# A bidirectional mLSTM scan: units of two, scores in banks of their own, and three small operations for five

## The chip, the cores and the metric

The kernel is one launch on all 8 cores of one Trainium2 chip. Each core works on one sample sequence of 2048 tokens and four prompt sequences of 256 tokens. The metric is the device time of the slowest core in microseconds (us). An execution is called slow when one die (cores 0 to 3, or 4 to 7) falls behind at a lower granted clock; only fast runs are compared, or cores of an undisturbed die. TensorE is PE in the profile, VectorE is DVE, ScalarE is ACT, GpSimd is POOL.

## The reference, cut to what matters

The layer has a Hyena branch, an mLSTM branch and an MLP. The change touches the mLSTM branch alone, and there one step of its scan over chunks of 128 tokens, for each of four heads and two directions:

```python
def step(carry, inp):
    C, n, m = carry
    ...                                            # gates: b, d, m_inter, m_comb
    s = jnp.einsum('bhjd,bhsd->bhjs', qc, kc) * jnp.exp(d - m_comb[..., None])
    num = w_inter[..., None] * jnp.einsum('bhjk,bhkv->bhjv', qc, C) + jnp.einsum('bhjs,bhsv->bhjv', s, vc)
    den = w_inter * jnp.einsum('bhjk,bhk->bhj', qc, n) + jnp.sum(s, axis=-1)
    h = num / jnp.maximum(jnp.abs(den), jnp.exp(-m_comb))[..., None]
    ...                                            # m_new, w_state, decay
    C_new = decay[..., None, None] * C + jnp.einsum('bhsk,bhsv->bhkv', kc * w_state[..., None], vc)
    n_new = decay[..., None] * n + jnp.einsum('bhs,bhsk->bhk', w_state, kc)
    return (C_new, n_new, m_new), h
```

The forward and the backward result are added. A chain of such steps (C to C_new) is serial, but the eight chains of a sequence are independent of each other.

## The kernel before: the parts concerned

A "pair" is one head in one direction. A group of the scan holds two heads of the sample sequence (4 pairs, 16 chunks; two such large groups) or eight pairs of prompt sequences (2 chunks; four small groups). That makes 192 steps in all, done four pairs at a time: 48 rounds. A round, with arguments cut and comments added:

```python
for i in range(nck):
    for batch in batches:                       # four pairs
        for p, (c_, d) in enumerate(batch):     # X = XB[p], Z = ZB[p]: two PSUM banks for each pair
            ... matmul(X[:, 0:128], lhsT=kT, rhs=qT)                # scores
        for e in st:
            ... vector.scalar_tensor_tensor(out=ST, in0=X[:, 0:128], WSq, masks)
            ... scalar.activation(out=cbt, in_=cf, scale=DECq)      # Cb: the state, decayed, bf16
            ... scalar.activation(out=kw, in_=ktok, scale=WSq)
        for e in st:
            ... matmul(X[:, 128:385], lhsT=ST, rhs=vt)              # output and denominator
            ... matmul(X[:, 128:385], lhsT=qT, rhs=cbt)
            ... matmul(X[:, 386:390], lhsT=kw, rhs=vt[:, c, 255:257])
            ... matmul(Z, lhsT=kw, rhs=vt)                          # the new part of the state
        for e in st: ... vector: cf[0:256] = cf * DECq + Z          # Cf, 128x512
        for e in st: ... vector: cf[256] = cf * DECq + X[...]       # Cf, last column
        for e in st: ... vector: sc0 = X[:, 384] * U                # the five small ones
        for e in st: ... vector: sc3 = max(-sc0, sc0)
        for e in st: ... vector: sc1 = max(sc3, EN)
        for e in st: ... vector: sc2 = 1 / sc1
        for e in st: ... vector: sc3 = sc2 * U
        for e in st:
            if first touch of this chunk: ... scalar.activation(out=hacc, in_=X[:, 128:384], scale=sc3)
            else:                         ... vector: hacc = X[:, 128:384] * sc3 + hacc
```

A helper puts in every wait by buffer, and a PSUM bank is one buffer. In the first half of a sequence's chunks the accumulate (Hacc) is a first touch and runs on ScalarE; in the second half the other direction has been there, and it runs on VectorE.

## Time and profile before

| | before |
|---|---|
| median, lowest, highest | 5136.06, 5121.35, 5364.1 us in 3 runs |
| spans of the 8 cores in the profiled run | 5090.8 to 5120.6 us |
| busy share of the whole span: PE, DVE, ACT | 65%, 41%, 20% |
| scan of a large group (16 rounds) | about 164.5 us |
| scan of a small group (4 rounds) | about 41 us |
| from the first scan's start to the last one's end, over the cores | 845 to 869 us |

A group's scan is counted from its first ST to the end of its last Hacc, in the timeline; the six together take some 494 us. Between groups lie the transposes of the next heads, and the norm and the store of the last ones. The shares of the whole span say little here, as nine tenths of it belong to other stages.

### The profile page before, as it was taken

How to read it: one execution, taken by the hardware profiler on the slowest of the kernel's cores; microseconds unless marked ns; L12 is line 12 of the kernel's file. 1: busy time of each engine (PE TensorE's matmuls, PEld its weight loads, DVE VectorE, ACT ScalarE, POOL GpSimd, SP SyncE). 2: the span in 40 equal slices, each digit the busy share in tenths (PEclk: the TensorE clock that was granted, in tenths of full speed). 3: DMA queues.
4: the chain of work that ended last, by engine and by line, in shares of the span. 5: the costliest groups of instructions: out<-in, count | busy, mean ns of one | idle time of the engine just before them, and what ended most of it. 6: DMA issues, size and time to landing. Idle time of an engine off the chain costs nothing.

```text
span 5120.6 us, 56640 instructions; the slowest of 8 cores (5090.8 to 5120.6 us)
## 1 busy us (share of the span) xinstructions
PE 3353.6 (65%) x17932; PEld 1732.5 (34%) x17932; DVE 2108.2 (41%) x4215; ACT 1019.2 (20%) x1859; POOL 413.8 (8%) x449
## 2 busy tenths in 40 slices
PE   2199999905444222289938586476864795698697
PEld 1144444403222111034414454335452342343343
DVE  0332201474656343354354555454432522532532
ACT  0401132215454222132010000000000221131131
POOL 0000000000000000000003232232310000000000
PEclk7599999956666555589958788788887898899898
DMA  8444543202020332235624353354436445445542
GB/s 144 143 98 135 179 136 99 83 16 71 17 75 17 57 38 38 50 108 170 180 94 155 127 163 133 127 163 150 147 133 177 78 74 157 98 67 122 123 68 65
DMA packets 316514, 547.68 MB, mean 107 GB/s; under 512 B 31190, under 2 KB 238457, under 8 KB 305785
## 3 DMA queue, kind: packets, MB, share of 16 engines
q1 hardware_dynamic: 221424, 442.73, 27.6%
q0 software_dynamic: 94800, 101.34, 13.0%
q8 instruction: 151, 2.47, 0.2%
q14 instruction: 139, 1.14, 0.1%
HBM read 521.56 MB, written 123.76 MB: 126 GB/s over the span
## 4 chain that ended last, share of the span: by engine, by line
PE 58%; DMA 15%; DVE 14%; ACT 6%; issue 5%; SPq 2%; POOL 1%; DVEq 0%; ACTq 0%; POOLq 0%
PE bank L538 11%; PE bank L1151 7%; PE bank L1372 7%; PE bank L1387 6%; PE bank L1244 6%; DMA ogP<-s_kvo 4%; PE bank L1220 4%; PE bank L1223 3%; PE bank L565 3%; DMA ust<-s_uT 2%; SPq L151 2%; DMA ptD<-pos 2%; DMA GTc<-GTS 2%; PE bank L1354 2%; DMA wada<-w_ada 2%
## 5 line engine op out<-in xcount | busy, mean ns | idle before, releaser
L538 PE MATMUL bank<-hnT,wsl 128*128 128x512 bf16 x2688 | 580.3, 379 | 0.0
L1244 PE MATMUL bank<-GTc,Y 128*128 128x256 bf16 x3328 | 412.6, 288 | 202.4 <-DMA GTc<-GTS 130.2
L1244 PEld LDWEIGHTS bank<-GTc,Y 128*128 128x128 bf16 x3328 | 340.2, 103 | 268.2 <-issue 209.0
L538 PEld LDWEIGHTS bank<-hnT,wsl 128*128 128x128 bf16 x2688 | 262.9, 98 | 317.3 <-issue 0.4
L1151 PE MATMUL bank<-HWb,FTf 128*128 128x512 bf16 x1568 | 357.2, 385 | 3.9 <-DMA FTf<-FTP 3.9
L1372 PE MATMUL bank<-mh,wslD 128*128 128x512 bf16 x1536 | 337.8, 384 | 7.3 <-DVE mh L467 7.3
L1387 PE MATMUL bank<-wslD,f1T 128*128 128x512 bf16 x1536 | 332.0, 379 | 6.3 <-DVE f1T L1376 6.3
L1025 PE MATMUL bank<-identb,hf 128*128 128x128 bf16 x192 | 35.7, 288 | 374.9 <-DVE hf L1020 347.4
L1220 PE MATMUL bank<-ztok,FTc 128*128 128x512 bf16 x832 | 205.2, 397 | 67.3 <-DMA FTc<-FTP 34.1
L1208 ACT COPY ztok<-bank 128x512 bf16<-128x512 bf16 x96 | 54.7, 588 | 951.7 <-PE bank L1206 949.3
L1338 PE MATMUL bank<-f1T,wslD 128*128 128x512 bf16 x384 | 100.3, 408 | 180.4 <-DVE tA L1344 104.1
L1151 PEld LDWEIGHTS bank<-HWb,FTf 128*128 128x128 bf16 x1568 | 154.0, 99 | 187.4 <-issue 12.5
L1372 PEld LDWEIGHTS bank<-mh,wslD 128*128 128x128 bf16 x1536 | 151.5, 99 | 193.0 <-issue 15.8
L1387 PEld LDWEIGHTS bank<-wslD,f1T 128*128 128x128 bf16 x1536 | 150.1, 98 | 188.3 <-issue 7.7
L1376 DVE TENSOR_TENSOR f1T<-tA 128x512 bf16<-128x512 f32 x192 | 132.9, 692 | 179.3 <-ACT tA L1375 177.6
L1223 PE MATMUL bank<-ztok,FTc 128*128 128x512 bf16 x832 | 197.7, 386 | 0.0
L1248 DVE SCALAR_TENSOR_TENSOR itmp<-zc,bfm,bank 128x256 f32<-128x256 bf16 x192 | 90.9, 479 | 250.5 <-PE bank L1244 234.5
L1375 ACT ACTIVATE tA<-bank,bfm 128x512 f32<-128x512 f32 x192 | 131.9, 687 | 227.4 <-DVE f1T L1376 179.9
L957 DVE SCALAR_TENSOR_TENSOR Cf<-Cf,TSC,bank 128x512 f32<-128x512 f32 x192 | 141.5, 748 | 81.5 <-PE bank L951 60.7
L565 PE MATMUL bank<-wsl,hnT 128*128 128x512 bf16 x768 | 165.9, 379 | 0.0
L1153 DVE TENSOR_TENSOR hss<-bank,invt 128x512 bf16<-128x512 f32 x112 | 76.7, 687 | 216.5 <-PE bank L1151 215.6
L936 ACT ACTIVATE Cb<-Cf,TSC 128x514 bf16<-128x514 f32 x192 | 136.8, 713 | 77.7 <-DVE Cf L962 77.7
(228 smaller groups left out, 4441.4 us busy)
## 6 DMA issues: line engine op xcount, KB each, us to landing
FTf<-FTS SPq DMA_DIRECT2D x96, 512.0 KB, 3.8
FTc<-FTS SPq DMA_DIRECT2D x96, 512.0 KB, 4.5
GTc<-GTS SPq DMA_DIRECT2D x32, 1536.0 KB, 8.5
wslD<-w_mlp POOLq DMA_DIRECT2D x48, 1024.0 KB, 9.4
s_uT<-stF SPq DMA_DIRECT2D x24, 1536.0 KB
ust<-s_uT SPq DMA_DIRECT2D x24, 1024.0 KB
wsl<-w_in POOLq DMA_DIRECT2D x18, 1024.0 KB, 12.1
wada<-w_ada POOLq DMA_DIRECT2D x6, 2048.0 KB, 23.1
```

Of the source, the lines that this page charges most:

```text
L538: op("pe", lambda: nc.tensor.matmul(pp[:], lhsT=wt[:, k, m * 128:(m + 1) * 128], rhs=hnT[:, k, tt * 512:(tt + 1) * 512], start=(k == 0), s ...
L565: op("pe", lambda: nc.tensor.matmul(pp[:], lhsT=hnT[:, k, tk * 128:(tk + 1) * 128], rhs=wt[:, k, :], start=(k == 0), stop=(k == 7)), r=[wb ...
L936: op("act", lambda: nc.scalar.activation(out=cbt[:], in_=cf[:], func=AF.Copy, scale=S(DECq)), r=[cfb, TSC_b], w=[cbb])
L957: op("dve", lambda: nc.vector.scalar_tensor_tensor(out=cf[:, :, 0:256], in0=cf[:, :, 0:256], scalar=Sx(e, DECq), in1=Z[:, 0:512].rearrange ...
L1151: op("pe", lambda: nc.tensor.matmul(ps[:], lhsT=ft[:, tc * 128:(tc + 1) * 128], rhs=HW_[:, tc, :], start=(tc == 0), stop=(tc == nt - 1)), ...
L1220: op("pe", lambda: nc.tensor.matmul(pr_[:], lhsT=fre[:, tc * 128:(tc + 1) * 128], rhs=ztok[:, tc, :], start=(tc == 0), stop=(tc == nt - 1) ...
L1223: op("pe", lambda: nc.tensor.matmul(pi_[:], lhsT=fim[:, tc * 128:(tc + 1) * 128], rhs=ztok[:, tc, :], start=(tc == 0), stop=(tc == nt - 1) ...
L1244: op("pe", lambda: nc.tensor.matmul(ps[:, 0:256], lhsT=Y[:, fc, j * 128:(j + 1) * 128], rhs=gt[:, fc * 256:(fc + 1) * 256], start=(fc == 0 ...
L1372: op("pe", lambda: nc.tensor.matmul(ps[:], lhsT=w1t[:, k, m4 * 128:(m4 + 1) * 128], rhs=mh[:, k, ts_], start=(k == 0), stop=(k == 7)), r=[ ...
L1375: op("act", lambda: nc.scalar.activation(out=ta[:], in_=ps[:], func=AF.Relu, bias=bfm[:, BM1 + fc:BM1 + fc + 1]), r=[psb, bfm_b], w=[tab])
L1376: op("dve", lambda: nc.vector.tensor_tensor(out=f1T[:, fc, ts_], in0=ta[:], in1=ta[:], op=ALU.mult), r=[tab], w=[f1T_b])
L1387: op("pe", lambda: nc.tensor.matmul(ps[:], lhsT=f1T[:, fbk * 8 + q, i * 128:(i + 1) * 128], rhs=w2t[:, q, :], start=first, stop=last), r=[ ...
```

## The change

Its intent is to break the ring in which every engine waits for another. Scores move into two banks of their own, so that they needn't wait for the last reader of the output bank; a unit becomes two pairs; output banks alternate from one unit to the next; and the front part of unit k+1 (scores, ST, Cb, kw) is given to the engines ahead of the back part of unit k. Besides, the factor U of the small operations is taken into the floor EN beforehand, which is the same function of the same numbers: 1/max(|x|·U, EN)·U = 1/max(|x|, EN/U).

```diff
-        op("dve", ... tensor_tensor(out=FREE[:], in0=R3[:], in1=R7[:], op=ALU.add) ...)
+        op("dve", ... tensor_tensor(out=V3(FREE), in0=V3(R3), in1=bc(ML), op=ALU.add) ...)
...
-                for i in range(nck):
-                    for batch in batches:
-                        ... X=XB[p], Z=ZB[p] ...
-                        ... matmul(X[:, 0:128], ...)
+                PB = 2
+                units = [(i, pairs[b:b + PB]) for i in range(nck) for b in range(0, len(pairs), PB)]
+                def stage1(k):      # scores
+                        bp = (k % 2) * PB + p
+                        ... X=XB[bp], Z=ZB[p], S=(ZB[2 + k % 2], p * 128) ...
+                            ... matmul(S[:, s0:s0 + 128], ...)
+                def stage2(st):     # ST; all Cb; all kw
+                def stage3(st):     # the back part's matmuls
+                def stage4(st):     # Cf, last column, then
+                        ... tensor_scalar(out=sc[:, 0:1], in0=X[:, 384:385], scalar1=-1.0, op0=ALU.mult)
+                        ... scalar_tensor_tensor(out=sc[:, 1:2], in0=X[:, 384:385], scalar=EN, in1=sc[:, 0:1], op0=ALU.max, op1=ALU.max)
+                        ... reciprocal(out=sc[:, 3:4], in_=sc[:, 1:2])
+                        ... Hacc as before
+                cur = stage1(0)
+                stage2(cur)
+                for k in range(len(units)):
+                    nxt = stage1(k + 1) if k + 1 < len(units) else None
+                    stage3(cur)
+                    yield
+                    if nxt is not None:
+                        stage2(nxt)
+                    stage4(cur)
+                    yield
+                    cur = nxt
```

More of the change, by code (lines that the diff above doesn't have):

```diff
@@ L799, in _phaseB @@
         op("act", lambda: nc.scalar.activation(out=R2[:], in_=R2[:], func=AF.Exp), r=[R2b], w=[R2b])
-        op("dve", lambda: nc.vector.tensor_tensor(out=FREE[:], in0=R3[:], in1=R7[:], op=ALU.add), r=[R3b, R7b], w=[FREEb])
+        op("dve", lambda: nc.vector.tensor_tensor(out=V3(FREE), in0=V3(R3), in1=bc(ML), op=ALU.add), r=[R3b, ML_b], w=[FREEb])
         op("act", lambda: nc.scalar.activation(out=FREE[:], in_=FREE[:], func=AF.Exp, scale=-1.0), r=[FREEb], w=[FREEb])
@@ L910, in run_groups @@
                 pairs = [(c_, d) for c_ in ctx for d in range(2)]
-                batches = [pairs[b:b + bsz] for b in range(0, len(pairs), bsz)]
-                for i in range(nck):
-                    for batch in batches:
-                        st = []
-                        for p, (c_, d) in enumerate(batch):
-                            js, h, s_ = c_["js"], c_["h"], c_["s"]
-                            c = i if d == 0 else nck - 1 - i
-                            cg = c_["t0"] // 128 + c
-                            col = d * 4 + h
-                            ri = rot[0] % NR; rot[0] += 1
-                            e = dict(c=c, cg=cg, col=col, tk=slice(c * 128, (c + 1) * 128), X=XB[p], Z=ZB[p], ST=STs[ri], kw=kws[ri], sc=scs[ri],
-                                     cf=Cf[js][d], cb=Cb[js][d], s=s_, c_=c_, d=d)
-                            st.append(e)
-                            qT, qTb = s_["qT"]; kT, kTb = s_["kT"]
-                            X, Xb = e["X"]
-                            for dk in range(2):
-                                op("pe", lambda: nc.tensor.matmul(X[:, 0:128], lhsT=kT[:, dk, e["tk"]], rhs=qT[:, dk, e["tk"]], start=(dk == 0), stop=(dk == 1)),
-                                   r=[kTb, qTb], w=[Xb], inc=(dk == 1))
-                        yield
-                        for e in st:
-                            S = lambda q: TSC[:, e["cg"], q, e["col"]:e["col"] + 1]
-                            X, Xb = e["X"]; ST, STb = e["ST"]; kw, kwb = e["kw"]; cf, cfb = e["cf"]; cbt, cbb = e["cb"]
-                            ktok, ktokb = e["s"]["ktok"]
-                            op("dve", lambda: nc.vector.scalar_tensor_tensor(out=ST[:], in0=X[:, 0:128], scalar=S(WSq), in1=masks[:, e["d"], :],
-                                                                             op0=ALU.mult, op1=ALU.mult), r=[Xb, TSC_b, masks_b], w=[STb])
-                            op("act", lambda: nc.scalar.activation(out=cbt[:], in_=cf[:], func=AF.Copy, scale=S(DECq)), r=[cfb, TSC_b], w=[cbb])
-                            op("act", lambda: nc.scalar.activation(out=kw[:], in_=ktok[:, e["c"], :], func=AF.Copy, scale=S(WSq)), r=[ktokb, TSC_b], w=[kwb])
-                        yield
-                        for e in st:
-                            X, Xb = e["X"]; Z, Zb = e["Z"]; ST, STb = e["ST"]; kw, kwb = e["kw"]; cbt, cbb = e["cb"]
-                            qT, qTb = e["s"]["qT"]; vt, vtb = e["s"]["vt"]
-                            c = e["c"]
-                            op("pe", lambda: nc.tensor.matmul(X[:, 128:385], lhsT=ST[:], rhs=vt[:, c, :], start=True, stop=False), r=[STb, vtb], w=[Xb], inc=False)
-                            for dk in range(2):
-                                op("pe", lambda: nc.tensor.matmul(X[:, 128:385], lhsT=qT[:, dk, e["tk"]], rhs=cbt[:, dk, :], start=False, stop=(dk == 1)),
-                                   r=[qTb, cbb], w=[Xb], inc=False)
-                            for dk in range(2):
-                                op("pe", lambda: nc.tensor.matmul(X[:, 386 + 2 * dk:388 + 2 * dk], lhsT=kw[:, dk * 128:(dk + 1) * 128], rhs=vt[:, c, 255:257], start=True, stop=True),
-                                   r=[kwb, vtb], w=[Xb], inc=(dk == 1))
-                            for dk in range(2):
-                                op("pe", lambda: nc.tensor.matmul(Z[:, dk * 256:(dk + 1) * 256], lhsT=kw[:, dk * 128:(dk + 1) * 128], rhs=vt[:, c, 0:256], start=True, stop=True),
-                                   r=[kwb, vtb], w=[Zb], inc=(dk == 1))
-                        yield
-                        Sx = lambda e, q: TSC[:, e["cg"], q, e["col"]:e["col"] + 1]
-                        for e in st:
-                            X, Xb = e["X"]; Z, Zb = e["Z"]; cf, cfb = e["cf"]
-                            op("dve", lambda: nc.vector.scalar_tensor_tensor(out=cf[:, :, 0:256], in0=cf[:, :, 0:256], scalar=Sx(e, DECq),
-                                                                             in1=Z[:, 0:512].rearrange("p (k v) -> p k v", v=256),
-                                                                             op0=ALU.mult, op1=ALU.add), r=[Zb, TSC_b, cfb], w=[cfb])
-                        for e in st:
-                            X, Xb = e["X"]; cf, cfb = e["cf"]
-                            op("dve", lambda: nc.vector.scalar_tensor_tensor(out=cf[:, :, 256:257], in0=cf[:, :, 256:257], scalar=Sx(e, DECq),
-                                                                             in1=X[:, 386:390].rearrange("p (k v) -> p k v", v=2)[:, :, 1:2],
-                                                                             op0=ALU.mult, op1=ALU.add), r=[Xb, TSC_b, cfb], w=[cfb])
-                        for e in st:
-                            X, Xb = e["X"]; sc, scb = e["sc"]
-                            op("dve", lambda: nc.vector.tensor_scalar(out=sc[:, 0:1], in0=X[:, 384:385], scalar1=Sx(e, Uq), scalar2=None, op0=ALU.mult),
-                               r=[Xb, TSC_b], w=[scb])
-                        for e in st:
-                            sc, scb = e["sc"]
-                            op("dve", lambda: nc.vector.scalar_tensor_tensor(out=sc[:, 3:4], in0=sc[:, 0:1], scalar=-1.0, in1=sc[:, 0:1],
-                                                                             op0=ALU.mult, op1=ALU.max), r=[scb], w=[scb])
-                        for e in st:
-                            sc, scb = e["sc"]
-                            op("dve", lambda: nc.vector.tensor_scalar(out=sc[:, 1:2], in0=sc[:, 3:4], scalar1=Sx(e, ENq), scalar2=None, op0=ALU.max),
-                               r=[scb, TSC_b], w=[scb])
-                        for e in st:
-                            sc, scb = e["sc"]
-                            op("dve", lambda: nc.vector.reciprocal(out=sc[:, 2:3], in_=sc[:, 1:2]), r=[scb], w=[scb])
-                        for e in st:
-                            sc, scb = e["sc"]
-                            op("dve", lambda: nc.vector.tensor_scalar(out=sc[:, 3:4], in0=sc[:, 2:3], scalar1=Sx(e, Uq), scalar2=None, op0=ALU.mult),
-                               r=[scb, TSC_b], w=[scb])
-                        for e in st:
-                            X, Xb = e["X"]; sc, scb = e["sc"]
-                            c_, c = e["c_"], e["c"]
-                            hacc, haccb = c_["hacc"], c_["haccb"]
-                            if c not in c_["touched"]:
-                                c_["touched"].add(c)
-                                op("act", lambda: nc.scalar.activation(out=hacc[:, c, :], in_=X[:, 128:384], func=AF.Copy, scale=sc[:, 3:4]),
-                                   r=[Xb, scb], w=[haccb])
-                            else:
-                                op("dve", lambda: nc.vector.scalar_tensor_tensor(out=hacc[:, c, :], in0=X[:, 128:384], scalar=sc[:, 3:4], in1=hacc[:, c, :],
-                                                                                 op0=ALU.mult, op1=ALU.add), r=[Xb, scb, haccb], w=[haccb])
@@ new lines, in run_groups @@
+                PB = 2
+                units = [(i, pairs[b:b + PB]) for i in range(nck) for b in range(0, len(pairs), PB)]
+                Sx = lambda e, q: TSC[:, e["cg"], q, e["col"]:e["col"] + 1]
+                def stage1(k):
+                    i, batch = units[k]
+                    st = []
+                    for p, (c_, d) in enumerate(batch):
+                        js, h, s_ = c_["js"], c_["h"], c_["s"]
+                        c = i if d == 0 else nck - 1 - i
+                        cg = c_["t0"] // 128 + c
+                        col = d * 4 + h
+                        ri = rot[0] % NR; rot[0] += 1
+                        bp = (k % 2) * PB + p
+                        e = dict(c=c, cg=cg, col=col, tk=slice(c * 128, (c + 1) * 128), X=XB[bp], Z=ZB[p], S=(ZB[2 + k % 2], p * 128), ST=STs[ri], kw=kws[ri], sc=scs[ri],
+                                 cf=Cf[js][d], cb=Cb[js][d], s=s_, c_=c_, d=d)
+                        st.append(e)
+                        qT, qTb = s_["qT"]; kT, kTb = s_["kT"]
+                        (S, Sb), s0 = e["S"]
+                        for dk in range(2):
+                            op("pe", lambda: nc.tensor.matmul(S[:, s0:s0 + 128], lhsT=kT[:, dk, e["tk"]], rhs=qT[:, dk, e["tk"]], start=(dk == 0), stop=(dk == 1)),
+                               r=[kTb, qTb], w=[Sb], inc=(dk == 1))
+                    return st
@@ new lines, in stage2 @@
+                def stage2(st):
+                    for e in st:
+                        (S, Sb), s0 = e["S"]; ST, STb = e["ST"]
+                        op("dve", lambda: nc.vector.scalar_tensor_tensor(out=ST[:], in0=S[:, s0:s0 + 128], scalar=Sx(e, WSq), in1=masks[:, e["d"], :],
+                                                                         op0=ALU.mult, op1=ALU.mult), r=[Sb, TSC_b, masks_b], w=[STb])
+                    for e in st:
+                        cf, cfb = e["cf"]; cbt, cbb = e["cb"]
+                        op("act", lambda: nc.scalar.activation(out=cbt[:], in_=cf[:], func=AF.Copy, scale=Sx(e, DECq)), r=[cfb, TSC_b], w=[cbb])
+                    for e in st:
+                        kw, kwb = e["kw"]; ktok, ktokb = e["s"]["ktok"]
+                        op("act", lambda: nc.scalar.activation(out=kw[:], in_=ktok[:, e["c"], :], func=AF.Copy, scale=Sx(e, WSq)), r=[ktokb, TSC_b], w=[kwb])
@@ new lines, in stage3 @@
+                def stage3(st):
+                    for e in st:
+                        X, Xb = e["X"]; Z, Zb = e["Z"]; ST, STb = e["ST"]; kw, kwb = e["kw"]; cbt, cbb = e["cb"]
+                        qT, qTb = e["s"]["qT"]; vt, vtb = e["s"]["vt"]
+                        c = e["c"]
+                        op("pe", lambda: nc.tensor.matmul(X[:, 128:385], lhsT=ST[:], rhs=vt[:, c, :], start=True, stop=False), r=[STb, vtb], w=[Xb], inc=False)
+                        for dk in range(2):
+                            op("pe", lambda: nc.tensor.matmul(X[:, 128:385], lhsT=qT[:, dk, e["tk"]], rhs=cbt[:, dk, :], start=False, stop=(dk == 1)),
+                               r=[qTb, cbb], w=[Xb], inc=False)
+                        for dk in range(2):
+                            op("pe", lambda: nc.tensor.matmul(X[:, 386 + 2 * dk:388 + 2 * dk], lhsT=kw[:, dk * 128:(dk + 1) * 128], rhs=vt[:, c, 255:257], start=True, stop=True),
+                               r=[kwb, vtb], w=[Xb], inc=(dk == 1))
+                        for dk in range(2):
+                            op("pe", lambda: nc.tensor.matmul(Z[:, dk * 256:(dk + 1) * 256], lhsT=kw[:, dk * 128:(dk + 1) * 128], rhs=vt[:, c, 0:256], start=True, stop=True),
+                               r=[kwb, vtb], w=[Zb], inc=(dk == 1))
@@ new lines, in stage4 @@
+                def stage4(st):
+                    for e in st:
+                        X, Xb = e["X"]; Z, Zb = e["Z"]; cf, cfb = e["cf"]
+                        op("dve", lambda: nc.vector.scalar_tensor_tensor(out=cf[:, :, 0:256], in0=cf[:, :, 0:256], scalar=Sx(e, DECq),
+                                                                         in1=Z[:, 0:512].rearrange("p (k v) -> p k v", v=256),
+                                                                         op0=ALU.mult, op1=ALU.add), r=[Zb, TSC_b, cfb], w=[cfb])
+                    for e in st:
+                        X, Xb = e["X"]; cf, cfb = e["cf"]
+                        op("dve", lambda: nc.vector.scalar_tensor_tensor(out=cf[:, :, 256:257], in0=cf[:, :, 256:257], scalar=Sx(e, DECq),
+                                                                         in1=X[:, 386:390].rearrange("p (k v) -> p k v", v=2)[:, :, 1:2],
+                                                                         op0=ALU.mult, op1=ALU.add), r=[Xb, TSC_b, cfb], w=[cfb])
+                    for e in st:
+                        X, Xb = e["X"]; sc, scb = e["sc"]
+                        op("dve", lambda: nc.vector.tensor_scalar(out=sc[:, 0:1], in0=X[:, 384:385], scalar1=-1.0, scalar2=None, op0=ALU.mult),
+                           r=[Xb], w=[scb])
+                    for e in st:
+                        X, Xb = e["X"]; sc, scb = e["sc"]
+                        op("dve", lambda: nc.vector.scalar_tensor_tensor(out=sc[:, 1:2], in0=X[:, 384:385], scalar=Sx(e, ENq), in1=sc[:, 0:1],
+                                                                         op0=ALU.max, op1=ALU.max), r=[Xb, TSC_b, scb], w=[scb])
+                    for e in st:
+                        sc, scb = e["sc"]
+                        op("dve", lambda: nc.vector.reciprocal(out=sc[:, 3:4], in_=sc[:, 1:2]), r=[scb], w=[scb])
+                    for e in st:
+                        X, Xb = e["X"]; sc, scb = e["sc"]
+                        c_, c = e["c_"], e["c"]
+                        hacc, haccb = c_["hacc"], c_["haccb"]
+                        if c not in c_["touched"]:
+                            c_["touched"].add(c)
+                            op("act", lambda: nc.scalar.activation(out=hacc[:, c, :], in_=X[:, 128:384], func=AF.Copy, scale=sc[:, 3:4]),
+                               r=[Xb, scb], w=[haccb])
+                        else:
+                            op("dve", lambda: nc.vector.scalar_tensor_tensor(out=hacc[:, c, :], in0=X[:, 128:384], scalar=sc[:, 3:4], in1=hacc[:, c, :],
+                                                                             op0=ALU.mult, op1=ALU.add), r=[Xb, scb, haccb], w=[haccb])
```

## The prediction

> **What bounds the kernel now.** I first read the slices, to see which part of the span the change lies in. The changed loop (the mLSTM scan) runs from 1204 us to 2075 us, slices 9 to 16 of 128 us each.
>
> ```profile
> PE   2199999905444222289938586476864795698697
> DVE  0332201474656343354354555454432522532532
> ACT  0401132215454222132010000000000221131131
> PEclk7599999956666555589958788788887898899898
> ```
>
> In those slices nobody is busy for even 80%. So the scan has no bound engine; it waits on itself. Where exactly, the waits of its first stretch (164 us, first two heads, 16 rounds of four head-directions, "pairs") say:
>
> ```profile
> DVE ST L934 <- PE bank L927: 41.7, 25, 31.5
> ACT Cb L936 <- DVE Cf L962: 38.8, 7, 6.3
> PE bank L927 <- ACT Hacc L990: 35.6, 24, 4.3
> ACT Hacc L990 <- DVE sc L982: 35.1, 8, 5.5
> PE bank L927 <- DVE Hacc L993: 32.4, 21, 4.4
> DVE Cf L957 <- PE bank L951: 23.4, 40, 1.0
> ```
>
> Read it as a ring: the score matmul L927 of a round waits for the last read (Hacc) of the round before, because it writes the same PSUM bank; ST waits for the score matmul, Cf for the state matmul, Cb for Cf, Hacc for the small scalars. Every engine stands still for tens of us out of 164, in turn. The busy columns of the same stretch (PE, PE loads, VectorE, ScalarE) confirm it: the busiest engine, VectorE, has 122.6 of 164 us.
>
> ```profile
> 1204.50:1368.50 164.00, 91.22 (x576) 54.23 (x576) 122.55 (x541) 79.97 (x161) 0.00 (x0) 0.67 0.02 4
> ```
>
> The timeline of VectorE over one round (start, length) gives the prices; start to start is what counts, as consecutive instructions overlap:
>
> ```profile
> 1298.47 1.12 DVE L934 SCALAR_TENSOR_TENSOR ST<-bank,TSC,masks 128x128 bf16<-128x128 f32 x4
> 1300.42 0.75 DVE L957 SCALAR_TENSOR_TENSOR Cf<-Cf,TSC,bank 128x512 f32<-128x512 f32 x1 [0.83 <-PE bank L951]
> 1301.55 0.75 DVE L957 SCALAR_TENSOR_TENSOR Cf<-Cf,TSC,bank 128x512 f32<-128x512 f32 x1 [0.38 <-PE bank L951]
> 1302.68 1.41 DVE L957 SCALAR_TENSOR_TENSOR Cf<-Cf,TSC,bank 128x512 f32<-128x512 f32 x2 [0.38 <-PE bank L951]
> 1304.00 0.59 DVE L962 SCALAR_TENSOR_TENSOR Cf<-Cf,TSC,bank 128x2 f32<-128x2 f32 x4
> 1304.51 0.59 DVE L967 TENSOR_SCALAR sc<-bank,TSC 128x1 f32<-128x1 f32 x4
> 1305.01 0.36 DVE L971 SCALAR_TENSOR_TENSOR sc<-sc 128x1 f32<-128x1 f32 x4
> 1305.31 0.57 DVE L975 TENSOR_SCALAR sc<-sc,TSC 128x1 f32<-128x1 f32 x4
> 1305.80 0.40 DVE L979 RECIPROCAL sc<-sc 128x1 f32<-128x1 f32 x4
> 1306.14 0.58 DVE L982 TENSOR_SCALAR sc<-sc,TSC 128x1 f32<-128x1 f32 x4
> 1306.63 2.05 DVE L993 SCALAR_TENSOR_TENSOR Hacc<-bank,sc,Hacc 128x256 f32<-128x256 f32 x4
> 1308.60 1.12 DVE L934 SCALAR_TENSOR_TENSOR ST<-bank,TSC,masks 128x128 bf16<-128x128 f32 x4
> ```
>
> A round lasts 10.13 us here, in the second half of the chunks, where Hacc is on VectorE; in the first half it is on ScalarE and a round takes 10.1 to 10.5 us. There are 16 rounds in each of two large groups and 4 in each of four small ones: 48 in all. By the score and Hacc times in the timeline the groups' scans last 165.6, 164.3 and about 41 us four times: 494 us, 9.6% of the span. Nothing outside them changes, so this is the most that is at stake.
>
> **What the Trainium skill says.** "PSUM — Partial Sum Buffer", section "PSUM bank collisions raise a hardware error": two engines may not touch the same bank and quadrant at once, whichever bytes; so software must wait by bank. That is why scores in columns 0 to 127 of a bank must wait for Hacc reading columns 128 to 383; the L927 waits above (35.6 + 32.4 us) are that wait. "Perfetto Trace Analysis", section "Matmuls", advises rotating independent matmul groups through banks so that evacuation overlaps the next group's matmuls. The change does that. "ScalarE: Activation LUTs", section "What ACT_TABLE_LOAD costs": 186 ns + 0.833 ns per element, about 93 ns more per pointer operand, back-to-back overlap of about 93 ns. The trace agrees: Cb, 514 wide with one pointer, by that 707 ns, measured 713; kw, 256 wide, 492 against 494; Cb to kw starts 0.61 us apart. "TensorE: Matmul & The Clock Gate", Part 1: the array runs at half clock after an idle window of about 3.4 us. Here the L943 to L945 matmuls of 257 columns follow 0.21 us apart, half speed, for three pairs of a round and faster only in the last. The clock column says 0.67.
>
> **The change part by part.**
> (1) Ring cut. Scores get banks of their own (two, alternating), output banks alternate between units, the unit shrinks to two pairs, and PE and VectorE/ScalarE are given unit k+1's front part before unit k's back part. The state for unit k+1 belongs to another head, so Cb of k+1 needs only Cf of unit k-1. The score waits and the Cf-to-Cb waits go; what remains is the busiest engine, or the longest ring over two units.
> (2) Small operations. Uq is folded into the floor: two of six small VectorE operations per pair go (the abs, 0.075 us start to start, and one TENSOR_SCALAR, 0.125). 192 pairs by 0.2 us is 38 us of VectorE. The FREE operation in the gate preparation keeps its shape; I put it at 0.
>
> VectorE per unit of two pairs, from the timeline: ST 2 x 0.27 = 0.54; Cf 2 x 0.66 = 1.32; its last column 2 x 0.125 = 0.25. The three small ones left depend on each other, with only one instruction in between instead of three: a dependent pair of tiny operations in the gate preparation starts 0.25 us apart for a length of 0.15, so length + 0.1. That gives 0.31 + 0.31 + 0.26 = 0.88 us to the first Hacc. Hacc 2 x 0.49 = 0.98. Sum with Hacc on VectorE: 3.97 us. Without it: 0.54 + 1.32 + 0.25 + 0.79 = 2.90 us.
>
> ScalarE per unit: Cb 2 x 0.61, kw 2 x 0.40, together 2.0 us; with Hacc (four in 1.97 us, so two about 0.95) 2.95 us.
>
> PE per unit: 1.13 us per pair at half clock for the back part, 0.22 for the scores: 2.7 us.
>
> The ring that stays when Hacc is on ScalarE, because Hacc of unit k-1 stands in ScalarE's queue before Cb of k+1: Cf start to the reciprocal's end 2.35, to Hacc 0.1, two Hacc 0.9, two Cb 1.22, first kw 0.49, kw to the next Cf start through PE 1.0 (1216.66 + 0.50 to 1218.15 in the timeline): 6.06 us for two units, 3.03 each. So a unit should take about 3.1 us in the first half, with all three engines nearly full, and 4.0 in the second, bound by VectorE. Two units are an old round: 6.2 and 8.0 against 10.3 and 10.1.
>
> Sum. Large group: fill 2.7 us (two Cb, one kw, PE), then 16 x 3.1 + 16 x 4.0 = 113.6; 116.3 us against 165, saved 48.6, twice: 97 us. Small group: 2.7 + 4 x 3.1 + 4 x 4.0 = 31.1 against 41, saved 10, four times: 40 us. Together 137 us. The groups' prologues and epilogues, closed by DMA waits for ogP of 10 to 17 us, run after the scan and wait for its end, so they move forward and swallow nothing. The change is serial time removed from a chain: 5136 - 137 = 4999 us, and I take 4998.
>
> **The rivals.**
> (a) The coupling is worse than the sums: with three engines within 7% of each other in the first half, semaphore delays and half-clock matmuls could make 3.5 and 4.4 us. Then a large group takes 129 us and a small one 34, saved 72 + 28 = 100 us: 5036, just inside 2%. For it: each hand-over costs 0.1 to 0.2 us above. Against: the order of issue puts the front part first everywhere.
> (b) It goes better: TensorE, hardly idle, holds full clock, and own-engine waits hide. VectorE alone then gives 2.8 and 3.7 us: 107 us per large group, saved 160 in all: 4976.
> (c) The scan is hidden behind something (loads of the next group, the ogP transfer), and the gain vanishes: 5136. Against: DMA busy is 2% in that stretch, and the next loads are issued only after it.
> (d) Halving the batch loses: more hand-overs of two instead of four, with the ring not really cut, since Z stays single per pair. Unit 5 us, no gain. Against: Z is freed by the first VectorE operation of the back part, 2.6 us before the next Cf.
>
> **Range and chances.** Rival (a) sets the upper side, (b) the lower; adding some noise of the kernel before (5121 and 5136 in its undisturbed runs) I take 4960 to 5045. 2% is 103 us, three quarters of my sum, so faster by over 2% has 0.78, within 2% 0.21, slower 0.01.
>
> **What would show it.** Right: windows of the two large scans near 116 us; the waits of L927 on Hacc gone; VectorE busy share above 90% there; 3.1 and 4.0 us from one unit's Cf to the one after next's, halved. ScalarE idle only in the second halves. Wrong: Cf still waiting for PE 0.4 us each or more (then PE's clock or kw was the bound), small operations further apart than 0.31 us, or epilogues that grew by what the scan lost.

## The result, and the profile after

The changed kernel is right and takes 5006.2 us in the median of 13 runs (4981.56 to 5503.58, slow ones among them); the kernel before, run beside it, 5136.06 in 15. The ratio of the fast runs is 0.9716, with a 95% interval of 0.9684 to 0.9747. The seven fast runs have a mean of 4988 us, some 146 us below the kernel before by that ratio. Ratios here are the mean time of one kernel's fast runs over that of the other's fast runs of the same rounds, so not quite the ratio of the medians. The profiled run is a fast one, with spans of 4956.9 to 5004.6 us. Two later controls of the same kernel gave 0.9719 and 0.9724.

| from the timelines of all cores | before | after | saved | predicted |
|---|---|---|---|---|
| large group's scan | 164.5 | 115.6 | 48.9, twice | 48.6, twice |
| small group's scan | 41 | 30.6 | 10.4, four times | 10, four times |
| sum of the six | | | 139 | 137 |
| first scan's start to last one's end (mean) | 854 | 716 | 138 | |

That the last two rows agree to 1 us is partly chance. In the two later controls the scans are the same (355 us together), but the stretch from the first to the last took 708 and 695 us: the gaps between groups differ by some 20 us from one execution to another.

The slices of the whole span after, VectorE's line, 125 us to a digit:

```profile
DVE  0322210475766333543355454454423522622632
```

The first large scan of this core lies in slices 9 and 10 (counted from 0), and fills them only in part. VectorE stood at 4 and 6 tenths there and now stands at 5 and 7. The finer view is two windows of equal length over the first large scan on core 1 (Hacc passes from ScalarE to VectorE at about 1263 us, a little before the second window starts); the columns are length, then busy time of PE, PE loads, VectorE, ScalarE and GpSimd with instruction counts, then clock, DMA share and GB/s:

```profile
1207.66:1266.00 58.34, 39.20 (x341) 26.57 (x342) 53.80 (x212) 53.73 (x111) 0.00 (x0) 0.88 0.06 16
1266.00:1324.20 58.20, 33.25 (x238) 23.50 (x235) 55.52 (x205) 30.68 (x64) 0.00 (x0) 0.67 0.00 1
```

Before, the busiest engine had 122.55 of 164.00 us, three quarters (core 2). Now VectorE has 92% of the first stretch and 95% of the second; ScalarE has 92% of the first and, with Hacc gone to VectorE, 53% of the second. The scan has a bound engine at last. The costliest waits of the compute engines of that core from 1209 to 1331 us (us in total, times, longest; TensorE's waits for issue and the rest are left out):

```profile
ACT Cb L942 <- DVE Cf L971: 23.9, 13, 2.2
...
PE bank L952 <- DVE ST L938: 18.2, 14, 2.2
...
PE bank L957 <- ACT kw L945: 9.8, 17, 0.6
...
ACT Hacc L991 <- DVE sc L984: 2.2, 3, 1.6
```

The two waits of the score matmul for Hacc are gone, and those of VectorE came down to some 4 us within the scan: what stands in the list are engines that wait for VectorE, or for ScalarE. Idle time of an engine that isn't the bound costs nothing. The timeline of VectorE over one unit of the second half shows why nothing is left there (start, length):

```profile
1293.25 1.40 DVE L966 SCALAR_TENSOR_TENSOR Cf<-Cf,TSC,bank 128x512 f32<-128x512 f32 x2
1294.57 0.41 DVE L971 SCALAR_TENSOR_TENSOR Cf<-Cf,TSC,bank 128x2 f32<-128x2 f32 x2
1294.89 0.22 DVE L976 TENSOR_SCALAR sc<-bank 128x1 f32<-128x1 f32 x2
1295.14 0.34 DVE L980 SCALAR_TENSOR_TENSOR sc<-bank,TSC,sc 128x1 f32<-128x1 f32 x2
1295.46 0.29 DVE L984 RECIPROCAL sc<-sc 128x1 f32<-128x1 f32 x2
1295.73 1.07 DVE L994 SCALAR_TENSOR_TENSOR Hacc<-bank,sc,Hacc 128x256 f32<-128x256 f32 x2
1296.72 0.60 DVE L938 SCALAR_TENSOR_TENSOR ST<-bank,TSC,masks 128x128 bf16<-128x128 f32 x2
1297.24 1.40 DVE L966 SCALAR_TENSOR_TENSOR Cf<-Cf,TSC,bank 128x512 f32<-128x512 f32 x2
```

No line carries an idle time in brackets, and Cf starts 3.99 us after Cf: the 3.97 us of the prediction's sum. In the first half Hacc starts on ScalarE at 1214.50, 1217.46 and 1220.62: a unit takes 2.96 and 3.16 us. From Cf to Cf over both large scans of all cores, the mean unit is 3.08 us in the first half and 3.99 in the second.

Could it be TensorE at a low clock instead? Over the second halves of the first large scan the granted clock ran from 0.56 to 0.72 on the cores of this run and its two controls, and the unit took 3.99 us on every one of them. So the second half doesn't follow TensorE's clock. The first half may follow it a little: 3.11 us at 0.91 (core 0), 3.03 at 0.98 (core 7).

### The profile page after: what moved, and what is told of

The parts are those of the page before. It is cut to its first block, busy times and chain, and to the rows that moved or that the text cites. A ratio compares the mean times of both kernels' runs of the same rounds, so it can differ in the third digit from the quotient of the medians.

```text
span 5004.6 us, 55578 instructions; the slowest of 8 cores (4956.9 to 5004.6 us)
## 1 busy us (share of the span) xinstructions
PE 3311.2 (66%) x17932; PEld 1724.6 (34%) x17932; DVE 2066.9 (41%) x3831; ACT 1019.8 (20%) x1859; POOL 413.1 (8%) x449
## 4 chain that ended last, share of the span: by engine, by line
PE 56%; DMA 16%; DVE 12%; ACT 6%; issue 5%; SPq 2%; POOL 1%; DVEq 0%; ACTq 0%; POOLq 0%
PE bank L538 12%; PE bank L1164 7%; PE bank L1385 7%; PE bank L1400 7%; PE bank L1257 6%; DMA ogP<-s_kvo 4%; PE bank L1233 4%; PE bank L1236 3%; PE bank L565 3%; DMA ust<-s_uT 2%; SPq L151 2%; DMA ptD<-pos 2%; PE bank L1367 2%; DMA wada<-w_ada 2%; DVE ctmp L1203 2%
## 5 line engine op out<-in xcount | busy, mean ns | idle before, releaser
L1385 PEld LDWEIGHTS bank<-mh,wslD 128*128 128x128 bf16 x1536 | 151.2, 99 | 191.7 <-issue 13.6
L452 ACT ACTIVATE yst<-xtD 128x1024 f32<-128x1024 f32 x24 | 25.3, 1054 | 624.8 <-DVE xtD L1371 623.2
L1038 PEld LDWEIGHTS bank<-identb,hf 128*128 128x128 bf16 x192 | 13.1, 104 | 397.6 <-issue 397.6
```

The source lines that it names most:

```text
L1385: op("pe", lambda: nc.tensor.matmul(ps[:], lhsT=w1t[:, k, m4 * 128:(m4 + 1) * 128], rhs=mh[:, k, ts_], start=(k == 0), stop=(k == 7)), r=[ ...
```

## The experiments

The theory: the time comes from the scan alone, the ring is cut by banks and order of issue together, and VectorE is what bounds the scan now. The rivals: the small operations alone did it; the banks alone, or the order alone, would have done it; the smaller unit is what helps. The runs on the two parts and on banks and order were made on one chip, those on the size of the unit, on GpSimd and the first control on a second, the last two on a third; the kernel before ran beside them on each. Every kernel gives a right result.

**The two parts one at a time.** First the small operations alone, in the kernel before:

```diff
-  FREE = R3 + R7;  sc: U*x, abs, max EN, reciprocal, *U
+  FREE = R3 + ML;  sc: -x, max(x, EN, -x), reciprocal
```

> The old serial loop of four pairs with only the small operations folded (three in place of five per pair, the floor formula changed with them). My theory: they lie on the ring, so the whole of their time is saved: 0.8 to 1.0 us of a 10.2 us round, times 48 rounds, 38 to 48 us; about 5085 us, ratio 0.991. With the run of the ring cut alone the two gains should add up to the whole, 140 us. Rival 'the small operations were the gain': ratio 0.972.

Measured: ratio 0.9951 (0.9921 to 0.9981), from two fast runs. The scans took 149.7 and 37.5 us: 2 x 14.8 + 4 x 3.5, some 42 to 44 us saved in the scans, as expected. The time missed the expectation: 5108 us in the mean of the two against 5085. The mean core span of the fast runs fell by 37 us, the slowest core's time by 26. In the profile the gaps between groups, which end in waits for transfers, add up to 351 to 389 us, depending on the core (before: 354 to 378), and the slowest core is one with long gaps; why they were longer here is open.

Then the other part alone, the changed kernel with the five old operations:

```diff
-  FREE = R3 + ML;  sc: -x, max(x, EN, -x), reciprocal
+  FREE = R3 + R7;  sc: U*x, abs, max EN, reciprocal, *U
```

> The pipelined scan with the five old small VectorE operations per pair put back (ring cut alone). My theory: the ring cut is the larger part of the gain, and the small operations now lie on VectorE, which is nearly full. The chain from the first small operation to Hacc grows from 0.88 to about 1.44 us per unit, so a unit goes from 3.0 to about 3.45 us in the first half and from 4.0 to 4.55 us in the second; a large group's scan takes about 132 us in place of 116.5, and the whole about 5036 us, a ratio to the kernel before of 0.982. Rival 'the small operations were the gain': the ratio would be close to 1. Rival 'they are hidden by the pipelining': the ratio stays at 0.972.

Only one of its 8 runs was fast, 5047.7 us, against a mean of 5133.8 for the fast runs of before: 0.983, without an interval. The scans I read from the undisturbed die: 137 and 35.5 us, so 76 us less than before and 62 more than with both parts. I had expected 132 for a large one. The windows (columns as above) and the small operations of one unit, both of core 5, show where the time goes:

```profile
1210.00:1240.00 30.00, 21.38 (x145) 13.15 (x146) 29.64 (x130) 24.39 (x50) 0.00 (x0) 0.69 0.01 1
```

```profile
1221.71 0.34 DVE L976 TENSOR_SCALAR sc<-bank,TSC 128x1 f32<-128x1 f32 x2
1222.04 0.28 DVE L980 SCALAR_TENSOR_TENSOR sc<-sc 128x1 f32<-128x1 f32 x2
1222.30 0.34 DVE L984 TENSOR_SCALAR sc<-sc,TSC 128x1 f32<-128x1 f32 x2
1222.62 0.29 DVE L988 RECIPROCAL sc<-sc 128x1 f32<-128x1 f32 x2
1222.89 0.34 DVE L991 TENSOR_SCALAR sc<-sc,TSC 128x1 f32<-128x1 f32 x2
1223.15 0.60 DVE L938 SCALAR_TENSOR_TENSOR ST<-bank,TSC,masks 128x128 bf16<-128x128 f32 x2
```

VectorE is busy for 29.64 of 30 us: it is the bound in the first half too, at 3.6 to 3.7 us a unit. The five small operations start at 1221.71 and the next ST at 1223.15: 1.44 us for two pairs, just what the expectation had. What it missed is that the first half pays all of it: the mean unit, from Cf to Cf, is 3.7 us there, where I had 3.45, and 4.67 in the second half, where I had 4.55. The three of the changed kernel take 0.84, by its timeline above. So the two removed cost 0.60 us a unit, 0.30 a pair; the prediction had 0.2 a pair, from batches of four. In a batch of four they were indeed worth that: 42 us over 192 pairs is 0.22 each. In units of two the same two operations are worth 62 us, 0.32 each. That also says why the parts are more than additive: 76 + 42 = 118, the whole change saves 139, and the 20 us between are the higher price of the small operations in the smaller unit.

**Banks or order.** The changed kernel with the scores back in columns 0 to 127 of the output bank:

```diff
-  S=(ZB[2 + k % 2], p * 128)
+  S=(XB[bp], 0)
```

> The changed kernel with one thing undone: the scores go back into columns 0 to 127 of the unit's output bank (output banks still alternate, order of issue kept). My theory: the score matmul of unit k+1 stands ahead of the back part of unit k in TensorE's queue and must now wait for Hacc of unit k-1, so a unit becomes serial again: 0.14 + 0.23 + 1.1 + 0.17 us from Hacc to the next Cf and 3.4 us from Cf to the end of Hacc, 5.1 us per unit, 162 us per large group; about 5120 us, ratio 0.995 to 1.0, in spite of fewer small operations. Rival 'the order of issue alone does it': ratio stays near 0.972.

Measured: ratio 1.0121 (1.0093 to 1.0148); the scans 184.4 and 44.5 us. It is slower than the kernel before, and slower than I expected. The group of score matmuls in its profile (busy us, mean ns, then idle time before them with its releasers):

```profile
L931 PE MATMUL bank<-qT,kT 128*128 128x128 bf16 x256 | 45.4, 282 | 179.4 <-ACT Hacc L991 91.4 <-DVE Hacc L994 81.4 <-ACT ktok L906 6.6
```

The wait that the change removed is back with the bank. And the changed kernel with its banks, but without the look-ahead:

```diff
-  cur = stage1(0); stage2(cur)
   for k in range(len(units)):
-      nxt = stage1(k + 1); stage3(cur); yield; stage2(nxt); stage4(cur); yield; cur = nxt
+      cur = stage1(k); stage2(cur); stage3(cur); yield; stage4(cur); yield
```

> The changed kernel with the banks kept and only the order of issue undone: each unit's front part is issued after the back part of the unit before. My theory: [...]Cb of unit k+1 stands behind Hacc of unit k on ScalarE, and a unit takes about 6.1 us in the first half and 5.4 us in the second (ST, TensorE's 1.1 us and hand-overs no longer lie beside VectorE's work): 185 us per large group, about 5187 us, ratio 1.012, slower than before. Rival 'separate banks alone do it, the engines find their own overlap': ratio near 0.972.

Measured: ratio 1.0239 (1.0216 to 1.0262); the scans 200.3 and 50.6 us, where I had expected 1.012 and 185 us for a large one. The group of the large Cf there:

```profile
L966 DVE SCALAR_TENSOR_TENSOR Cf<-Cf,TSC,bank 128x512 f32<-128x512 f32 x192 | 143.8, 749 | 249.3 <-PE bank L960 237.9 <-ACT Cb L942 3.4 <-ACT junkB L1019 3.1
```

VectorE waits 237.9 us for TensorE, and the timeline shows the two kinds: before the first Cf of a unit about 3.0 us in the first half and 1.35 in the second, before the second Cf 0.38. The second kind is what I had left out of both estimates. In a serial unit the back part of a pair takes TensorE 1.13 us (granted clock 0.50 to 0.58 in both runs), Cf only 0.66, so the second Cf comes 0.47 us late, and the two Cf start 1.13 us apart in nearly every unit of both traces; 32 units by 0.47 is 15 us, as much as the whole miss of the last run and two thirds of that of the one before (the rest I did not trace). Each half of the ring cut alone loses to the kernel before, although both runs have the cheaper small operations; the two together win 76 us without them. The likely reason is that units of two double the number of hand-overs. That is argued and not shown: no run has units of four with one half of the cut, or with both.

**The size of the unit.** The changed kernel with one pair to a unit:

```diff
-  PB = 2
+  PB = 1
```

> The changed kernel with units of one pair in place of two, all else kept. My theory: two pairs side by side hide half of the wait between dependent small operations; with one, each waits for the one before (Cf 0.82 to its last column, then 0.12 + 0.25 + 0.31 + 0.27 us to Hacc), so a pair costs VectorE 2.57 us in the second half and the ring gives 2.2 us in the first: 5.1 and 4.4 us per two pairs. Large group about 155 us, small about 40 us, ratio about 0.995. Rival 'shorter units pipeline better': ratio under 0.972.

Measured: ratio 0.9924 (0.9889 to 0.9959), scans 152.8 and 39.2 us, as expected. Its small operations on VectorE, one pair to a line:

```profile
1231.77 0.15 DVE L976 TENSOR_SCALAR sc<-bank 128x1 f32<-128x1 f32 x1
1232.03 0.22 DVE L980 SCALAR_TENSOR_TENSOR sc<-bank,TSC,sc 128x1 f32<-128x1 f32 x1
1232.35 0.16 DVE L984 RECIPROCAL sc<-sc 128x1 f32<-128x1 f32 x1
1232.45 0.35 DVE L938 SCALAR_TENSOR_TENSOR ST<-bank,TSC,masks 128x128 bf16<-128x128 f32 x1
```

The dependent steps are 0.26 and 0.32 us apart for one pair, just as in the changed kernel for two: with one or two in a row a step costs the delay until a result can be read, not the work. (The ST behind them depends on none of them and starts after 0.10.) With one pair the delay is paid twice as often, and the hand-overs too. The edit has a side effect: with PB = 1 the units share one state bank and alternate between two output banks, where the changed kernel uses two and four. In the first large scan of core 1, TensorE waited 0.2 us for the state bank and 8.3 us for an output bank, beside 37 us lost. So the unit's size is the likely cause of most of the loss, but the fewer banks are not ruled out for the rest.

**The bound moved.** If VectorE bounds the second half, taking work from it there must shorten the unit from 4.0 to 3.0 us, whatever it costs elsewhere. In the second half ScalarE now scales a copy of the output, and GpSimd adds it:

```diff
-  vector: hacc = X[:, 128:384] * sc3 + hacc
+  scalar.activation(out=og2s[i % 2], in_=X[:, 128:384], func=AF.Copy, scale=sc3)
+  gpsimd.tensor_tensor(out=hacc, in0=og2s[i % 2], in1=hacc, op=ALU.add)
```

> The changed kernel with the accumulation of the second half taken off VectorE: ScalarE scales the output out of PSUM into an SBUF tile (as it does in the first half) and the idle GpSimd adds it to Hacc. My theory: VectorE is the bound of the second half (3.97 us a unit, 0.98 of it Hacc), so that half falls to the 3.0 us of the first: about 99 us per large group and 26 us per small one, 50 us off the changed kernel, ratio to the kernel before about 0.962. Rival 'TensorE at half clock is the bound of the second half' (2.7 us a unit of work and waits for Cf): no gain, 0.972. Rival: GpSimd's add (0.68 us for 128x256 elsewhere in this kernel) or its traffic slows VectorE: gain under 20 us.

The window of a second half on core 0 (columns as above), then two units, and the last add of the group:

```profile
1260.00:1298.00 38.00, 23.52 (x232) 16.52 (x232) 36.99 (x153) 36.05 (x78) 17.76 (x25) 1.00 0.01 2
```

```profile
1288.46 1.41 DVE L967 SCALAR_TENSOR_TENSOR Cf<-Cf,TSC,bank 128x512 f32<-128x512 f32 x2
...
1291.43 1.40 DVE L967 SCALAR_TENSOR_TENSOR Cf<-Cf,TSC,bank 128x512 f32<-128x512 f32 x2
...
1306.11 0.84 ACT L996 ACTIVATE og<-bank,sc 128x256 f32<-128x256 f32 x2 [2.07 <-DVE sc L985]
1306.72 1.59 POOL L998 TENSOR_TENSOR Hacc<-og,Hacc 128x256 f32<-128x256 f32 x2 [1.32 <-ACT og L996]
```

A unit takes 2.97 us in the second half as well: the bound was VectorE, as the theory says. (The granted clock rose too, to 1.00, but the changed kernel's second half didn't follow the clock, as shown above.) VectorE and ScalarE are now both near full (36.99 and 36.05 of 38). But with the end of GpSimd's last add counted, the scans took 102.5 and 29.5 us, not 99 and 26, and the ratio was 0.9697 (0.9659 to 0.9734) against 0.9719 (0.9696 to 0.9742) for the control of the changed kernel beside it, where 0.962 was expected. Against this control the mean core span of the fast runs is 20 us less, 4941 in place of 4961. The units gained 1 us each, but at the end of a group the last pair passes through ScalarE (0.84) and GpSimd (1.59) instead of one VectorE instruction of 1.07 us. From the last unit's Cf to the end of a large scan it is 5.26 us here and 3.55 in the changed kernel (medians over all cores), so this path makes 1.7 of the 3.5 us that a large scan lies above the expectation. Most of the rest is in the sum itself: units of 3.08 and 3.02 us in place of 3.0, and a start of 3.2 us in place of the 2.7 of the prediction's fill.

The control:

> The changed kernel itself, on the same chip and beside the same runs as the three that follow, so that they can be compared with it: ratio 0.972 as before, large groups' scans 115.6 us, small ones 30.6 us.

It measured 0.9719, with scans of 115.6 and about 30.7 us.

One step further, kw too goes to GpSimd in every unit:

```diff
-  scalar.activation(out=kw, in_=ktok, func=AF.Copy, scale=WSq)
+  gpsimd.tensor_scalar(out=kw, in0=ktok, scalar1=WSq, op0=ALU.mult)
```

> As the run before, and kw (the scaled keys) moved from ScalarE to GpSimd as well. My theory of the first half: VectorE 2.90, ScalarE 2.95 and the ring 3.03 us a unit stand close together. Taking 0.8 us from ScalarE and 0.49 us from the ring leaves VectorE's 2.90, so only about 0.1 us a unit is won, 10 us in all: ratio about 0.960. If ScalarE alone were the bound, a unit would fall to 2.3 us or so and 60 us more would go. If GpSimd is slow at this operation (over 0.8 us each), it becomes the bound and the run is slower than the one before.

The group of kw on GpSimd (busy us, mean ns, idle before):

```profile
L946 POOL TENSOR_SCALAR kw<-ktok,TSC 128x256 bf16<-128x256 bf16 x128 | 116.2, 922 | 405.1 <-ACT ktok L907 374.1 <-PE bank L961 22.7 <-PE bank L932 8.2
```

At 0.92 us each, with adds of 0.73, GpSimd needs 2 x 0.92 + 2 x 0.73 = 3.3 us a unit. It is the busiest engine of the second half (35.77 of 40 us from 1260 us on core 1), and a unit there takes 3.40 to 3.55 us; that it alone is the bound isn't shown, as TensorE and VectorE wait in turn too. The large scans took 107 to 109 us, worse than 102.5, the small ones 29.8; the ratio was 0.9694 (0.9662 to 0.9727), from three fast runs, where 0.960 was expected, and no different from the one without it. The run also answers what bounds the first half. There the unit fell only from 3.08 to 3.01 us, although ScalarE had lost 0.8 us of its work, and VectorE is busy for 29.33 of 30 us (core 1, from 1215 us). So ScalarE was not what bounded it.

Last, the tail mended: the last unit of each group keeps its one VectorE instruction, the others the split.

```diff
+  elif last unit of the group:
+      vector: hacc = X[:, 128:384] * sc3 + hacc
   else:
       scalar.activation(...); gpsimd.tensor_tensor(...)
```

> Control, the changed kernel unaltered, five rounds: 0.972 of the kernel before; large scans 115.6 us, small ones 30.6 us, mean core span of the fast runs 4961 us.

> The split accumulate (ScalarE scales a copy, GpSimd adds), but the last unit of each group keeps the one VectorE instruction. In the run with the split everywhere, large scans took 102.5 us and small ones 29.5 when the end of GpSimd's last add is counted: the end of a group lost what the units gained, since the final pair has to pass through ScalarE (0.84 us for two) and GpSimd (1.60) instead of VectorE (1.07). Theory that the tail is the loss: 1.2 us less per group, so large 101.3, small 28.3, and the mean core span of fast runs 27 us below the control's (20 for the split everywhere); ratio to the kernel before 0.966 to 0.969. Rival, that the gain is swallowed by the gaps between the groups (transfers) or by a clock that falls: scans shorter, mean core span within 10 us of the control's, ratio 0.970 to 0.972.

Measured: the scans 101.5 and 28.6 us, within 0.3 us of what was expected if the tail is the loss. The ratio was 0.9694 (0.9666 to 0.9722), the control's 0.9724 (0.9703 to 0.9745). The mean core span of its four fast runs is 4942 us, of the control's three 4958: 16 us less, where 27 were expected, and each of the four (4929 to 4952) lies under each of the three (4954 to 4961). For the slowest core it is 4971 against 4983, and the intervals overlap. So this version is faster on the mean core, but that it beats the changed kernel in the time that counts is not shown. Nor is it shown to beat the split everywhere, which had gained 20 us on the mean core over its own control, on another chip. Where the rest went can be followed part of the way: the six scans lost 37 us together, the stretch from the first to the last scan 25, so the gaps between groups gave back 12. These end in transfers, whose waits differ by more than that from core to core; which of them grew for what reason I leave open.

## Why the prediction was right

*The size.* I predicted 4998 us, range 4960 to 5045, faster at 0.78. The median was 5006.2, which is the slowest of the seven fast runs (4982 to 5006, mean 4988), and the ratio's interval of 0.9684 to 0.9747 lies wholly beyond 2%.

*The ring is the bound, and the scan is all that is at stake.* Right. The score's waits for Hacc are gone, they return with the shared bank (91.4 + 81.4 us), and the scans' 139 us appear as 138 us between the first scan's start and the last one's end. The waits for ogP grew, from 177 to 187 us in the mean over the cores, but the gaps between groups as a whole did not: 360 us before and after (353 and 340 in the controls). That the time fell by 146 us where the sum had 137 is within what the gaps differ by. One line of the evidence was misread: of the 41.7 us that ST waited for the score matmul, 31.5 are one wait that ended when the scan began, so ST's share of the ring was 10 us.

*Units of 3.1 and 4.0 us.* Right: 3.08 in the first half and 3.99 in the second, in the mean over the large scans of all cores. That 3.97 and 3.99 agree so well has some luck in it: the last column took 0.32 us where the sum had 0.25, and the small operations 0.04 less than it had. The sum over VectorE's instructions, start to start, was the tool that did it, and moving Hacc off VectorE confirmed the bound by making it 2.97.

*Steps of the small operations, 0.31 + 0.31 + 0.26 = 0.88.* Measured 0.25 + 0.32 + 0.27 = 0.84.

*TensorE at half clock, 2.7 us a unit.* Half right. In the second half the clock was 0.67 on core 1. In the first it was 0.88, better than I took it, as rival (b) had it; but VectorE and ScalarE were at 92% there, so it brought nothing beyond the 3.1 us.

*What was mis-sized.* The line "192 pairs by 0.2 us is 38 us of VectorE" priced the two removed operations in batches of four. That is right for the kernel before (42 us measured alone), but in the changed kernel they are worth 62 us. The total did not suffer, as the sum of a unit priced the three that stay by their own delays.

*The rivals.* (a) was too high: large scans of 129 us did not come. (b) gives 165 us by its own units, not the 160 it says. (c) fell, by the 138 us. (d) fell, though with a lesson: halving the batch with only one half of the ring cut does lose, 1.2% and 2.4%. Of the expectations for experiments, those two were 22 and 15 us too low for a large scan; some 15 us of each are the second Cf's wait for a half-clock TensorE, which they left out. That wait does not exist in the prediction's own sums, where TensorE runs ahead.

## What to carry to other kernels

Where every engine idles in turn, look for the ring first, and cut it whole: a buffer of its own for the front part and an order of issue that puts the next front part ahead of the last back part win together, and each alone can lose, here probably because the smaller unit that makes room for them doubles the hand-overs. Then price the new bound engine by start-to-start times over one unit; tiny dependent operations cost their delay, so fewer steps are worth more, the smaller the batch. When work is moved off the new bound engine, count the end of each group too, where the longer path is no longer hidden.

## What the Trainium skill lacked or had wrong

- "VectorE: DVE Perf Modes", section "The DRAIN you can't avoid", speaks of the flush between instructions, but gives no distance for tiny operations that depend on each other, and I found none in the other pages. Here they start 0.25 to 0.33 us apart, with one pair or two in a row, while independent ones follow after 0.08 to 0.13 in rows of four. Of the changed kernel's units of 3.1 and 4.0 us, 0.84 are such steps.
- "TensorE: Matmul & The Clock Gate", Part 1, ties half clock to an idle window of about 3.4 us, and full clock to a busy one of that length, without saying how busy. From 1270 to 1300 us in the changed kernel's core 1 the longest gap between recorded matmuls is 1.8 us, and the granted clock is 0.67; it is 1.00 from 1276.2 to 1282.9, with TensorE busy for 3.32 of 6.7 us, and 0.50 after that, until 1296.5, with TensorE busy for 9.32 of 13.6 us. With units of 3.0 us in place of 4.0, at a like busy share (23.52 of 38 us against 19.57 of 30), the clock was 1.00. The page's warning of short idles between groups of matmuls fits better than the window, but has no number to plan with.
- "GPSIMD Engine Reference", section 4.1 "Engine selection", calls one-input operations "roughly line-rate" and two-input ones about two times slower than on VectorE. Here a multiply of 256 bf16 elements by a scalar of each partition, one tensor in and one out, took 0.92 us on GpSimd, longer than the two-input add of 256 f32 elements, 0.73. (Spans on GpSimd are rough in this profile.)
